# A hybrid decoder layer on one core: an account that meters the adding DMAs, a reordered head, a norm stepped at half tiles, and gate sigmoids ahead of silu

## The chip, the cores and the metric

The kernel runs on one core of a Trainium2 chip. The metric is device time in microseconds (us), the median of several executions. TensorE (PE) multiplies matrices, VectorE (DVE) and ScalarE (ACT) work elementwise, GpSimd (POOL) does a few small operations and issues one kind of DMA, and SyncE (SP) issues nearly all other DMAs. Every engine takes its instructions in the order in which the program lists them, and waits for other engines by semaphores.

## The reference

One layer for 256 tokens of width 1024, in float32: an RMS norm and one wide input projection, which feeds two branches; a gated mix of the branches; cross attention over 256 memory tokens; a squared-ReLU MLP; a last RMS norm. Cut to what matters here:

```python
n = rmsnorm(x);  z = n @ w_in      # c_a, c_g, q, k, v, qi, ki, wi, gc, ga
u = c_a * sigmoid(c_g)
u = causal depthwise conv of u, 31 taps, + conv_b
y_conv = silu(layernorm(u) * ln_g + ln_b) @ w_conv_out
y_attn = attention(q, k, v over the 64 best keys by the qi, ki, wi index) @ w_attn_out
h = x + (sigmoid(gc) * y_conv + sigmoid(ga) * y_attn) @ w_mix_out
h = h + cross_attention(rmsnorm(h), rmsnorm(mem))     # keys mem @ wx_kv, 4 heads
h = h + relu(rmsnorm(h) @ w_ff1)**2 @ w_ff2;  out = rmsnorm(h)
```

## The kernel before, in words

**Precision.** Almost every product is made of three: weights and activations are each split into a high part, rounded to the matmul's type, and a low rest. A weight chunk of 128 x 2048 (1 MB, tile `raw`) comes from memory; for each half of it ACT copies the high part (`hi`) and DVE subtracts to get the low part (`lo`). One "tile" of work on PE uses one such half: 8 matmuls of high weights on 512 columns (high and low activations) and 8 of low weights on 256.

**Streams.** `STREAM` lists the weight chunks in the order of use. `load()` issues the DMA of the next one on SP; three buffers of `raw` (and one in another pool) hold chunks, and a buffer's next load is issued when its low parts are done.

**Order.** All instructions are put in order while the program is built. `Counted` keeps for each of PE, DVE and ACT a running sum of estimated prices (`pe.total`, `dve.total`, `scalar.total`), and the builder compares these sums to decide what to put in next. After each PE tile come `meanwhile()` (optional work), the tile's own evacuation, and `tick()`, which steps every generator in `chains` once and counts `nturn`. The generators are the index scores, the heads of the attention, the layer norm, the gate's sigmoids. In order the tiles are: memory keys (`xk`), four pairs of `conv`, `qi`, `ki`, four more pairs of `conv`, `gc` (8 tiles), `v` (8), `q` and `k` in turn (16), `ga` (8), `ao` (8), `co` (8), `mix` (8), then cross attention and the MLP. The matmuls of `co` need the layer norm's result `u2`.

**The convolution.** Its 31 taps are shared out. Tap 0 is ACT's. Some are scalar_tensor_tensor on DVE, put in one by one from `fill` where `dve.total` allows. The others are *adds*: `Group.products` makes two ACT products of u and a tap's weights into the tile `prod` (one slot for each of the four groups of two channel tiles), and POOL issues a DMA that adds the 256 KB slot to the tile `added`. `ADDED` says how many taps of each group go that way: 11, 11, 10, 10, so 42 adds in all. A group may make its next product 3 turns after its last one, and `meanwhile` tries twice, so up to two products go in per tile. The slot must have been read by the last DMA before ACT overwrites it. When a half's taps are in and 3 turns have passed since its last product, `Half.add` sums `acc` and `added`; after both halves `layer_norm` starts: mean by a matmul (`ps_mub`), squares, inverse root (`rsqrt`, with a POOL power), silu on ACT, and high and low parts of `u2`, the high ones by a DVE copy. It waits for all heads, and the sigmoids of `ga` wait for its silu.

**The head of the program.** The vector of gains and biases (`vec`, 36 KB) is loaded on ACT's queue; SP loads half of the transposed memory (`mem_t`), half of chunk 0, the other halves, then rows of `x` and chunk 1. DVE multiplies all eight slices of `mem_t` by a gain, and then come the first matmuls `xk`. Eight matmuls on zeros (`ps_warm`) run before. The memory's own norm (`memory()`) ends with a POOL power `rs_m` and, one turn later, a PE transpose of it into `ps_mrb`.

Of the kernel before, what the change touches and what calls it, by code (L numbers as in the profile page):

```python
# [16 lines left out]
P = 128  # L17
# [8 lines left out]
ADDED = (11, 11, 10, 10)  # L26
# [80 lines left out]
def block_kernel(ctx, tc, x, xt, mem, memt, wst, wki, vecs, convw, gout, out):  # L107
# [75 lines left out]
    nload = [0]  # L183
    high_jobs, low_jobs = [], []

    def load(parts=1, before=lambda q: None):
# [57 lines left out]
    chains, fill, turn, done = [], [], [0], []  # L244
# [11 lines left out]
    def meanwhile():  # L256
# [5 lines left out]
        for _ in range(2):  # L262
            for g in groups:
                if g.ready() and scalar.total + 800 < pe.total + AHEAD:
                    g.products()
                    groups.remove(g)
                    groups.append(g)
                    break
# [4 lines left out]

    def tick():
        for c in list(chains):
            if next(c, "end") == "end":
                chains.remove(c)
# [97 lines left out]
    nc.scalar.dma_start(vec, vecs)  # L375
# [33 lines left out]
    for j in range(8):  # L409
# [87 lines left out]
    def memory():  # L497
# [11 lines left out]
        yield  # L509
# [32 lines left out]
    class Group:  # L542
# [5 lines left out]
        def ready(self):  # L548
            return self.open and self.left and nturn[0] >= self.issued + 3
# [11 lines left out]
    class Half:  # L561
# [18 lines left out]
        def add(self):  # L580
# [175 lines left out]
    u2 = []  # L756
# [3 lines left out]
    def layer_norm():  # L760
# [19 lines left out]
        dve.tensor_tensor(out=vs[:, 0, :], in0=vs[:, 0, :], in1=vs[:, 1, :], op=ALU.add)  # L780
        yield
        yield
        rs = rsqrt(vs[:, 0, :], "vr")
        yield
        while len(headed) < NH:
            yield
        act(table, table, AF.Silu)
        rsb = spread(rs, "rsb").unsqueeze(1).to_broadcast([P, 2, S])
        for c, cs in enumerate(pairs):
            dve.tensor_tensor(out=acc[:, cs, :], in0=acc[:, cs, :], in1=rsb, op=ALU.mult)  # L790
            for t in (2 * c, 2 * c + 1):
                act(acc[:, t, :], acc[:, t, :], AF.Silu, scale=lng[:, t : t + 1], bias=lnb[:, t : t + 1])
            if c == 1:
                yield
        gates.append(True)
        for c in range(4):
            parts_of(pairs[c])
            normed.append(True)
            if c != 1:
                yield  # L800

    def parts_of(cs):
        hi = u2[0].hi(cs.start, 2)
        dve.tensor_copy(hi, acc[:, cs, :])
        dve.tensor_tensor(out=u2[0].lo(cs.start, 2), in0=acc[:, cs, :], in1=hi.bitcast(F32), op=ALU.subtract)
# [5 lines left out]
    def head(h, q, k):  # L811
# [19 lines left out]
        yield  # L831
        for qb in range(2):
# [14 lines left out]
        headed.append(h)  # L847
# [19 lines left out]
    def gate_sigmoid():  # L867
        while not gates:
            yield
        act(table, table, AF.Sigmoid)  # L870
        for c in range(4):
            cs = slice(2 * c, 2 * c + 2)
            act(ga_t[:, cs, :], ga_t[:, cs, :], AF.Sigmoid)
            if c == 1:
                yield

    for i in range(4):
# [492 lines left out]
```

## Time and profile before

| | before |
|---|---|
| median of 3 runs | 522.6 us (521.56 to 524.28) |
| the profiled execution, its span | 525.86 us, 524.1 us |
| PE, DVE, ACT, POOL busy | 96%, 78%, 62%, 9% |
| bytes read from memory | 92.21 MB |

An engine's busy share is the mean over the whole span; what a stage costs is read from the waits inside it. "Granted clock" is the share of TensorE's full clock (2.4 GHz) that the chip let it have: 0.5 is 1.2 GHz.

### The profile page before, as it was taken

To read this page: it belongs to the slowest core of one execution; us is meant where nothing else is said; L and a number is where in the kernel's file an instruction comes from. 1 tells how busy PE (TensorE), PEld (TensorE's weight loads), DVE (VectorE), ACT (ScalarE), POOL (GpSimd) and SP (SyncE) were. 2 spreads that over 40 slices of the span, in tenths; PEclk is the share of its full clock that TensorE was granted. 3 is DMA by queue.
4 is the path that set the end of the run, shared out by engine and by line. 5 is a ranking of instruction groups with operands and counts; after the bars stand their busy time and mean duration, and the time that the engine had idled before them with its cause. 6 is when DMAs were issued, how large, how long until landed. Compare 5 with 4: busy or idle time off the path is not lost.

```text
span 524.1 us, 7696 instructions
## 1 busy us (share of the span) xinstructions
PE 505.6 (96%) x2876; PEld 442.2 (84%) x2876; DVE 407.2 (78%) x786; ACT 327.2 (62%) x595; POOL 45.2 (9%) x65
## 2 busy tenths in 40 slices
PE   8999899999959999999999999999999999999994
PEld 6999899888848898888888888988888888888883
DVE  2698999999869999689999985769666556666554
ACT  2665867776687876759669566556655545554432
POOL 1001222233332110000000000000000000000000
PEclk9999999999988999999999999999999999999999
DMA  8757989999999974453754454345555554565302
GB/s 305 282 229 230 283 210 227 229 239 252 256 258 252 239 202 161 162 222 110 303 199 165 151 193 185 120 161 180 223 203 198 199 202 161 179 222 175 148 0 80
DMA packets 20901, 104.76 MB, mean 200 GB/s; under 512 B 2432, under 2 KB 3328, under 8 KB 10496
## 3 DMA queue, kind: packets, MB, share of 16 engines
q1 hardware_dynamic: 14384, 92.90, 50.7%
q0 software_dynamic: 6048, 11.01, 11.7%
q8 instruction: 22, 0.36, 0.3%
q10 hardware_dynamic: 432, 0.36, 0.2%
q14 instruction: 15, 0.12, 0.1%
HBM read 92.21 MB, written 1.05 MB: 178 GB/s over the span
## 4 chain that ended last, share of the span: by engine, by line
PE 56%; DVE 22%; DMA 13%; ACT 5%; issue 3%; POOL 0%; POOLq 0%; DVEq 0%; ACTq 0%; SPq 0%
PE ps_f L88 17%; PE ps_ff L88 16%; DMA added<-prod 10%; DVE lo L88 8%; PE ps_ga L88 4%; DVE acc L88 3%; PE ps_xk L88 3%; PE ps_xo L88 2%; PE ps_k L88 2%; PE ps_xv L88 2%; DVE score L88 2%; PE ps_xq L88 2%; PE ps_ao L88 2%; DMA raw<-in_wst_dram 1%; DVE h_t L88 1%
## 5 line engine op out<-in xcount | busy, mean ns | idle before, releaser
L88 DVE TENSOR_TENSOR lo<-raw,hi 128x1024 fp32r<-128x1024 f32 (+1 forms) x161 | 195.0, 1216 | 5.9 <-ACT hi L88 5.9
L88 ACT ACTIVATE hi<-raw 128x1024 fp32r<-128x1024 f32 (+1 forms) x161 | 167.8, 1048 | 22.5 <-PE ps_ff L88 18.4
L88 PE MATMUL ps_ff<-hi,fs 128*128 128x512 f32 x256 | 81.7, 391 | 0.0
L88 PE MATMUL ps_f<-ff,hi 128*128 128x512 f32 x256 | 64.9, 393 | 0.2 <-DVE ff L88 0.2
L88 DVE SCALAR_TENSOR_TENSOR acc<-u,cw,acc 128x253 f32<-128x253 f32 (+18 forms) x148 | 62.2, 467 | 0.2
L88 PEld LDWEIGHTS ps_ff<-hi,fs 128*128 128x128 f32 x256 | 48.1, 188 | 9.7
L88 DVE TENSOR_TENSOR ft<-ps_f,ft 128x256 f32<-128x256 f32 x32 | 13.6, 425 | 53.9 <-ACT ft L88 53.9
L88 PEld LDWEIGHTS ps_f<-ff,hi 128*128 128x128 f32 x256 | 46.7, 188 | 9.8 <-DVE ff L88 1.1
L88 PE MATMUL ps_ff<-lo,fs 128*128 128x512 f32 x128 | 50.0, 390 | 0.0
L88 ACT ACTIVATE prod<-u,cw 128x226 f32<-128x226 f32 (+10 forms) x84 | 36.1, 477 | 20.2 <-DMA added<-prod 20.2
L557 POOL DMA_DIRECT2D added<-prod x42 | 36.5, 870 | 128.8 <-ACT prod L88 50.5
L88 PE MATMUL ps_conv<-n,hi 128*128 128x256 f32 x256 | 46.7, 285 | 0.0
L88 PEld LDWEIGHTS ps_conv<-n,hi 128*128 128x128 f32 x256 | 39.9, 192 | 0.8 <-issue 0.7
L88 PEld LDWEIGHTS ps_f<-ff,lo 128*128 128x128 f32 x256 | 35.1, 190 | 2.5
L88 PE MATMUL ps_conv<-n,lo 128*128 128x256 f32 x128 | 36.2, 283 | 0.0
L88 PE MATMUL ps_f<-ff,lo 128*128 128x256 f32 x256 | 36.0, 282 | 0.0
L88 ACT ACTIVATE fs<-ft 128x256 fp32r<-128x256 f32 x32 | 13.4, 419 | 31.2 <-DVE ft L88 31.2
L88 PEld LDWEIGHTS ps_ff<-lo,fs 128*128 128x128 f32 x128 | 24.1, 188 | 4.5
L88 ACT ACTIVATE ft<-ps_f 128x256 f32<-128x256 f32 x32 | 12.2, 380 | 22.5 <-PE ps_f L88 21.4
L88 PEld LDWEIGHTS ps_conv<-n,lo 128*128 128x128 f32 x128 | 24.5, 192 | 0.0
L88 PE MATMUL ps_q<-n,hi 128*128 128x512 f32 x64 | 18.4, 434 | 3.6 <-DVE q L88 3.6
L88 PE MATMUL ps_v<-hi,n 128*128 128x512 f32 x64 | 19.9, 389 | 0.0
(229 smaller groups left out, 870.2 us busy)
## 6 DMA issues: line engine op xcount, KB each, us to landing
raw<-in_wst_dram SPq DMA_DIRECT2D x79, 1024.0 KB, 4.9
added<-prod POOLq DMA_DIRECT2D x42, 256.0 KB, 7.9
raw<-in_wst_dram SPq DMA_DIRECT2D x6, 512.0 KB, 9.4
mem_t<-in_memt_dram SPq DMA_DIRECT2D x2, 512.0 KB, 5.5
x_rm<-in_x_dram SPq DMA_DIRECT2D x2, 512.0 KB, 9.0
mem_rm<-in_mem_dram SPq DMA_DIRECT2D x1, 1024.0 KB, 7.8
mem_t<-in_memt_dram SPq DMA_DIRECT2D x1, 1024.0 KB, 6.9
h_t<-in_xt_dram SPq DMA_DIRECT2D x1, 1024.0 KB, 8.3
```

Source lines behind the costliest of these rows:

```text
L88: return fn(*args, **kwargs)
L557: nc.gpsimd.dma_start(added[:, ts, :].rearrange("p t n -> p (t n)"), prod[:, self.n, :, :].rearrange("p t n -> p (t n)"), accum_op=ALU.add)
```

## The change

1. **Fewer adds, metered.** `ADDED` becomes 11, 10, 9, 8. An account `dma` sums DMA time: 1.3 ns for each column of a weight load, 1600 for each add, and never below `pe.total - 3000`. `meanwhile` makes one product at most, and only while the account stands under `pe.total + 500`. A group waits 3 turns while the account is under `pe.total - 1000`, otherwise 4, and a half ends 5 turns after its last product.
2. **The head.** `vec` is SP's first load. Chunk 0 comes as 512, 512 and 1024 columns; `mem_t`'s second half stands behind the first two of these. The multiplies of `mem_t` stand between the first matmuls. Nine matmuls on zeros. The transpose of `rs_m` comes four turns after its power.
3. **The norm.** `layer_norm` is in a new list, `urgent`, which `tick` steps and which is stepped once more in the middle of a tile of `form_b`. Its waits are restated in half tiles. The high parts of `u2` are ACT copies.
4. **Sigmoids first.** A head counts as done after its reciprocal. The sigmoids of `ga` start then, pair by pair, and silu waits for them.
5. **Small moves.** The sum of `ao`'s two halves is put in later (`lazily`); the scaling of the keys `kx` moves from the `ao` stage to just before `xq`.

```diff
-ADDED = (11, 11, 10, 10)
+ADDED = (11, 10, 9, 8)
...
-    nload = [0]
+    nload, dma = [0], [0.0]
...
-    def load(parts=1, before=lambda q: None):
+    def load(cuts=(0, N_CHUNK), before=lambda q: None):
...
-        for q in range(parts):
+        for q, ns in enumerate(slice(a, min(b, n)) for a, b in zip(cuts, cuts[1:])):
             before(q)
-            ns = slice(q * n // parts, (q + 1) * n // parts)
             nc.sync.dma_start(raw[:, ns], src[:, ns])
+            dma[0] += 1.3 * (ns.stop - ns.start)
...
-        for _ in range(2):
-            for g in groups:
-                if g.ready() and scalar.total + 800 < pe.total + AHEAD:
-                    g.products()
...
+        dma[0] = max(dma[0], pe.total - 3000)
+        for g in groups:
+            if g.ready() and scalar.total + 800 < pe.total + AHEAD and dma[0] < pe.total + 500:
+                dma[0] += 1600
+                g.products()
...
+    def step(some):
+        for c in list(some):
+            if next(c, "end") == "end":
+                some.remove(c)
+
     def tick():
...
+        step(chains)
+        step(urgent)
...
                 pe.matmul(ps, w[0][:, kt, :], x2.both(kt), start=kt == first, stop=False, skip_group_check=True)
+            step(urgent)
             for kt in kts:
...
-    nc.scalar.dma_start(vec, vecs)
+    nc.sync.dma_start(vec, vecs)
...
-        nc.sync.dma_start(mem_t[:, 4 * q : 4 * q + 4, :], memt[:, 4 * q : 4 * q + 4, :])
-
-    load(2, load_memory)
-    load(2, load_rows)
-    load(2)
+        if q in (0, 2):
+            nc.sync.dma_start(mem_t[:, 2 * q : 2 * q + 4, :], memt[:, 2 * q : 2 * q + 4, :])
+
+    load((0, 512, 1024, 2048), load_memory)
+    load((0, 1024, 2048), load_rows)
+    load((0, 1024, 2048))
...
-    for j in range(8):
+    for j in range(9):
         nc.tensor.matmul(ps, zero_r[:, :P], zero_r, start=True, stop=True)
...
-    for kt in range(KT):
-        dve.tensor_scalar(mem_t[:, kt, :], mem_t[:, kt, :], g_mem[:, kt : kt + 1], None, ALU.mult)
     psk = [ps_mm(f"ps_xk0{ct}") for ct in range(2)]
     for ct in range(2):
         for kt in range(KT):
+            if ct == 0:
+                dve.tensor_scalar(mem_t[:, kt, :], mem_t[:, kt, :], g_mem[:, kt : kt + 1], None, ALU.mult)
             mem_keys(psk[ct], 0, ct, kt)
...
-        yield
+        for _ in range(4):
+            yield
         act(mrb, spread(rs_m, "mrb"), AF.Copy)
...
-            return self.open and self.left and nturn[0] >= self.issued + 3
+            return self.open and self.left and nturn[0] >= self.issued + (3 if dma[0] < pe.total - 1000 else 4)
...
-                    p.left or not p.open or not (now or nturn[0] >= p.issued + 3) for p in self.groups):
+                    p.left or not p.open or not (now or nturn[0] >= p.issued + 5) for p in self.groups):
...
-                start(layer_norm())
+                urgent.append(layer_norm())
...
         dve.tensor_tensor(out=vs[:, 0, :], in0=vs[:, 0, :], in1=vs[:, 1, :], op=ALU.add)
-        yield
-        yield
+        for _ in range(4):
+            yield
         rs = rsqrt(vs[:, 0, :], "vr")
         yield
-        while len(headed) < NH:
+        yield
+        while gating[0] in chains:
             yield
         act(table, table, AF.Silu)
...
+            act(u2[0].hi(cs.start, 2), acc[:, cs, :], AF.Copy)
+            ready.append(scalar.total + 100)
+            if c < 3:
                 yield
-        gates.append(True)
...
     def gate_sigmoid():
-        while not gates:
+        while len(headed) < NH:
             yield
         act(table, table, AF.Sigmoid)
         for c in range(4):
+            while len(gates) < 2 * c + 2:
+                yield
...
     def after_ao(ct, ps):
-        total(ya[:, ct, :], ps)
-        due.append(lambda: added_up.append(ct))
+        act(ya[:, ct, :], ps[:, S:], AF.Copy)
...
     sq_x.fold(True)
+    dve.tensor_tensor(out=kx, in0=kx, in1=mrb.unsqueeze(1).to_broadcast([P, XH, S]), op=ALU.mult)
     scaled = start(cross_scale())
```

## Rows read from the trace of the kernel before

**Rows 1.** From the page: busy time of PE with its share of the span, and the granted clock in 40 equal slices, in tenths.

```profile
PE 505.6 (96%) x2876; PEld 442.2 (84%) x2876; DVE 407.2 (78%) x786; ACT 327.2 (62%) x595; POOL 45.2 (9%) x65
PEclk9999999999988999999999999999999999999999
```

**Rows 2.** The list of PE's waits: who waited for whom, us in total, how often, the longest.

```profile
PE ps_q L88 <- DVE q L88: 3.6, 1, 3.6
PE ps_s L88 <- DVE k L88: 2.3, 1, 2.3
...
PE ps_mrb L88 <- POOL rs_m L508: 1.6, 1, 1.6
...
PE ps_mub L88 <- ACT ptr L88: 0.6, 1, 0.6
...
PE ps_xq L88 <- DVE cx L88: 0.3, 1, 0.3
```

**Rows 3.** Two stretches, the end of the `v` tiles and the `q` and `k` tiles behind them: the stretch, its length, busy us (and instructions) of PE, PEld, DVE, ACT and POOL, then the mean granted clock, the busy share of the DMA engines and GB/s.

```profile
118.00:146.00 28.00, 27.47 (x137) 23.14 (x135) 23.84 (x45) 18.67 (x34) 8.65 (x11) 1.00 1.04 261
149.00:161.00 12.00, 9.66 (x38) 8.14 (x39) 10.89 (x23) 8.34 (x18) 3.87 (x5) 0.72 1.02 230
```

**Rows 4.** The waits between 118 and 146 us (first row), then single instructions of ACT and of PE in order of time: start, us, the instruction, and in brackets the idle time before it and what ended it.

```profile
ACT prod L88 <- DMA added<-prod: 9.3, 6, 3.9
...
144.73 0.87 ACT L88 ACTIVATE prod<-u,cw 128x230 f32<-128x230 f32 x2 [3.92 <-DMA added<-prod]
145.50 1.06 ACT L88 ACTIVATE v_rm<-ps_v 128x512 f32<-128x512 f32 x2
...
133.94 0.39 PE L88 MATMUL ps_v<-hi,n 128*128 128x512 f32 x1
...
149.05 2.74 PE L88 MATMUL ps_q<-n,hi 128*128 128x512 f32 x8 [3.58 <-DVE q L88]
```

**Rows 5.** From the page: the two large DMA queues (SP's and POOL's: packets, MB, the time of the packets as a share of 16 engines' span), and the DMA issues of the adds (count, KB each, median us from issue to landing).

```profile
q1 hardware_dynamic: 14384, 92.90, 50.7%
q0 software_dynamic: 6048, 11.01, 11.7%
...
added<-prod POOLq DMA_DIRECT2D x42, 256.0 KB, 7.9
```

**Rows 6.** The adds by stretch: the stretch, its length, POOL's time in them and their number, the granted clock, the share of the DMA engines and GB/s.

```profile
96.00:118.00 22.00, 6.07 (x7) 1.00 0.97 243
118.00:146.00 28.00, 7.89 (x10) 1.00 1.04 261
```

**Rows 7.** The head: single instructions of ACT's queue, DVE and PE in order of time; two stretches of 4 us with PE's busy time and number of matmuls first; and from the page the landing of `vec` (KB, us).

```profile
0.74 0.41 ACTq L375 DMA_DIRECT2D vec<-in_vecs_dram  x1
...
5.09 1.14 DVE L88 TENSOR_SCALAR mem_t<-mem_t,vec 128x256 f32<-128x256 f32 x4 [3.23 <-DMA vec<-in_vecs_dram]
8.54 1.14 DVE L88 TENSOR_SCALAR mem_t<-mem_t,vec 128x256 f32<-128x256 f32 x4 [2.30 <-DMA mem_t<-in_memt_dram]
...
1.92 3.78 PE L410 MATMUL ps_warm<-zero_r 128*128 128x512 f32 x8 [1.92 <-DVE zero_r L395]
6.30 12.60 PE L88 MATMUL ps_xk<-mem_t,raw 128*128 128x256 f32 x48 [0.60 <-DVE mem_t L88]
...
6.30:10.30 4.00, 4.00 (x10) 3.20 (x11) 1.14 (x4) 0.00 (x0) 0.00 (x0) 1.00 0.96 360
10.30:14.30 4.00, 4.00 (x20) 3.54 (x19) 0.91 (x2) 1.81 (x3) 0.55 (x1) 1.00 1.02 415
...
vec<-in_vecs_dram ACTq DMA_DIRECT2D x1, 36.0 KB, 4.3
```

**Rows 8.** The memory's norm on POOL and PE, single instructions in order of time.

```profile
56.36 0.72 POOL L508 TENSOR_TENSOR rs_m<-ss_m,half 128x2 f32<-128x2 f32 x1 [1.93 <-DMA added<-prod]
...
57.13 0.43 PE L88 MATMUL ps_mrb<-ident,rs_m 128*128 128x128 f32 x2 [1.63 <-POOL rs_m L508]
```

**Rows 9.** Prices: four DVE taps in a row (start, us); then groups of equal instructions with their count, busy us and mean ns of one; and from the chain of waits in order of time two tiles of PE (start, us).

```profile
127.15 1.63 DVE L88 SCALAR_TENSOR_TENSOR acc<-u,cw,acc 128x249 f32<-128x249 f32 x4
...
L88 ACT ACTIVATE prod<-u,cw 128x226 f32<-128x226 f32 (+10 forms) x84 | 36.1, 477 | 20.2 <-DMA added<-prod 20.2
L88 DVE CAST u<-acc 128x512 fp32r<-128x512 f32 x4 | 1.7, 420 | 0.0
L88 DVE TENSOR_TENSOR kv<-kv,mrb 128x1024 f32<-128x1024 f32 x1 | 1.2, 1218 | 0.0
...
208.61 5.59 PE ps_ga L88 x32
```

**Rows 10.** The layer norm: single instructions of DVE, ACT and PE from the sum of the second half to the first matmul of `co`.

```profile
205.95 1.23 DVE L88 TENSOR_TENSOR acc<-acc,added 128x1024 f32<-128x1024 f32 x1
210.19 0.89 DVE L88 TENSOR_TENSOR usum<-usum 128x256 f32<-128x256 f32 x2
...
235.15 1.28 ACT L88 ACT_TABLE_LOAD   x1
...
247.52 0.69 DVE L88 TENSOR_TENSOR u<-acc,u 128x512 fp32r<-128x512 f32 x1
...
248.75 2.00 PE L88 MATMUL ps_co<-u,hi 128*128 128x512 f32 x8
```

**Rows 11.** DVE at the cross attention's scores, one instruction.

```profile
303.98 0.69 DVE L88 TENSOR_REDUCE xmx<-ps_xs 128x2 f32<-128x512 f32 x1 [1.08 <-PE ps_xs L88]
```

More of the change, by code (lines that the diff above doesn't have):

```diff
@@ L241, in weights @@
         return [w.rearrange("p (k n) -> p k n", k=kt) for w in prepared.pop(key)]
-    chains, fill, turn, done = [], [], [0], []
+    chains, urgent, fill, turn, done = [], [], [], [0], []
     waiting = [False]
@@ L261, in meanwhile @@
             later.pop(0)()
-        for _ in range(2):
-            for g in groups:
-                if g.ready() and scalar.total + 800 < pe.total + AHEAD:
-                    g.products()
-                    groups.remove(g)
-                    groups.append(g)
-                    break
+        dma[0] = max(dma[0], pe.total - 3000)
[3 more added lines that the diff above has]
+                g.products()
+                groups.remove(g)
+                groups.append(g)
+                break
         while may_fill() and dve.total < pe.total + AHEAD:
@@ L272, in meanwhile @@
             g.finish()
+    def step(some):
+        for c in list(some):
+            if next(c, "end") == "end":
+                some.remove(c)
     def tick():
-        for c in list(chains):
-            if next(c, "end") == "end":
-                chains.remove(c)
+        step(chains)
+        step(urgent)
         nturn[0] += 1
@@ L753, in block_kernel @@
         form_a("v", hf, n2, v_rm, (1.0, 1.0))
-    u2 = []
+    u2, gating = [], []
     normed = []
@@ L788, in layer_norm @@
         rsb = spread(rs, "rsb").unsqueeze(1).to_broadcast([P, 2, S])
+        ready = []
         for c, cs in enumerate(pairs):
             dve.tensor_tensor(out=acc[:, cs, :], in0=acc[:, cs, :], in1=rsb, op=ALU.mult)
+            scalar.after(dve.total + 100)
             for t in (2 * c, 2 * c + 1):
                 act(acc[:, t, :], acc[:, t, :], AF.Silu, scale=lng[:, t : t + 1], bias=lnb[:, t : t + 1])
-            if c == 1:
+            act(u2[0].hi(cs.start, 2), acc[:, cs, :], AF.Copy)
+            ready.append(scalar.total + 100)
+            if c < 3:
                 yield
-        gates.append(True)
-        for c in range(4):
-            parts_of(pairs[c])
-            normed.append(True)
-            if c != 1:
-                yield
[L802 to L805, printed above, removed]
+        for c, cs in enumerate(pairs):
+            for _ in range(4):
+                if pe.total < ready[c]:
+                    yield
+            dve.after(ready[c])
+            dve.tensor_tensor(out=u2[0].lo(cs.start, 2), in0=acc[:, cs, :], in1=u2[0].hi(cs.start, 2).bitcast(F32),
+                              op=ALU.subtract)
+            normed.append(True)
     o2 = Pair("o")
@@ L831, in head @@
         yield
+        headed.append(h)
         for qb in range(2):
@@ L871, in gate_sigmoid, with gate_attention @@
         for c in range(4):
+            while len(gates) < 2 * c + 2:
+                yield
             cs = slice(2 * c, 2 * c + 2)
             act(ga_t[:, cs, :], ga_t[:, cs, :], AF.Sigmoid)
-            if c == 1:
-                yield
+            yield
+    def gate_attention(ct, ps):
+        total(ga_t[:, ct, :], ps, bga[:, ct : ct + 1])
+        due.append(lambda: gates.append(ct))
+    gating.append(start(gate_sigmoid()))
     for i in range(4):
-        form_b("ga", i, n2, lambda ct, ps: total(ga_t[:, ct, :], ps, bga[:, ct : ct + 1]))
-    gating = start(gate_sigmoid())
+        form_b("ga", i, n2, gate_attention)
     for c in heads:
@@ L884, in block_kernel, with add, lazily @@
     memorised = start(memory_parts())
-    added_up = []
+    added_up, lazy = [], []
     def after_ao(ct, ps):
-        total(ya[:, ct, :], ps)
-        due.append(lambda: added_up.append(ct))
+        act(ya[:, ct, :], ps[:, S:], AF.Copy)
+        ready, turn_of = scalar.total + 100, nturn[0]
+        def add():
+            dve.after(ready)
+            dve.tensor_tensor(out=ya[:, ct, :], in0=ps[:, :S], in1=ya[:, ct, :], op=ALU.add)
+            added_up.append(ct)
+        lazy.append((ready, turn_of, add))
+    def lazily(force=False):
+        while lazy and (force or lazy[0][0] < max(dve.total, pe.total) or nturn[0] > lazy[0][1] + 2):
+            lazy.pop(0)[2]()
     def branches():
-        dve.tensor_tensor(out=kx, in0=kx, in1=mrb.unsqueeze(1).to_broadcast([P, XH, S]), op=ALU.mult)
-        while gating in chains:
+        while gating[0] in chains:
             yield
         for ct in range(KT):
+            lazily()
             while ct >= len(added_up):
                 yield
+                lazily()
             dve.tensor_tensor(out=ga_t[:, ct, :], in0=ya[:, ct, :], in1=ga_t[:, ct, :], op=ALU.mult)
@@ L905, in block_kernel @@
         form_b("ao", i, o2, after_ao)
+        lazily()
+    lazily(True)
     while fill:
```

3 lines of the change are left out of this document (1 added, 2 removed).

## The prediction

> **What bounds the kernel now.** I read the page first. PE is busy 96% of the span, and its granted clock is full but for two slices [rows 1]. So nothing but PE's idle time and its slow time can be won: 524.1 - 505.6 = 18.5 us idle, of which some 7 us are the tail behind the last matmul, which the change leaves alone.
>
> The second view is the list of PE's waits [rows 2]. Its two longest, 3.6 us for `q` and 2.3 us for `k`, are both for evacuations of the attention's projections. The third view is the stretch in which they lie: from 149 to 161 us the granted clock is 0.72, and the DMA engines are at 1.02 [rows 3]. At that clock (1 - 0.72) x 12 = 3.4 us are lost; the short idle pieces in it fall mostly at full clock, and I count 3.2. Together this place costs 3.6 + 2.3 + 3.2 = 9.1 us.
>
> The fourth view says why. Between 118 and 146 us ACT stood 9.3 us waiting to overwrite a `prod` slot that an add's DMA had not yet read, once for 3.92 us [rows 4]. The last matmul of `v` began at 133.94 us, yet ACT copied `v` out at 145.50, some 11 us later. PE ran four more tiles into free banks and then stood until the first `q` had been taken out, 149.05 us. The cause is DMA time. SP's queue took 50.7% of the span for 92.90 MB, so 0.507 x 524.1 / 92.90 = 2.86 us per MB, 3.0 us per chunk of 1.05 MB, 1.5 us per tile; the 42 adds took 0.117 x 524.1 / 42 = 1.46 us each [rows 5]. Two tiles of PE take 5.59 us [rows 9], so a tile leaves 2.8 - 1.5 = 1.3 us, room for 0.9 adds. In the ten tiles from 118 to 146 us ten adds went out, of which PE's idle time at the end is a part; the program had packed them into the eight tiles of `v` [rows 6]. Eight tiles have room for 7.
>
> **Part 1, adds.** Products per tile fall from at most two to one, in `v` from 10 to at most 8. The excess over the room falls from (10 - 7) x 1.46 = 4.4 us of DMA time to 1.5. With four groups taking turns a slot is reused after four tiles, 11.2 us, against a median of 7.9 us from issue to landing [rows 5]. In `q` and `k`, 38 - 12 - 7 - 8 = 11 adds are left (12 went out before the row at 96 us, 7 in it) for 16 tiles, which have room for 14. So ACT's lag of 11 us should shrink by about 9.3 - 1.5 = 7.8 us, to 3 to 4 us, and PE bears four tiles of lag before it stands. I take 8.8 of the 9.1 us as won. The bounds are 9.1 and 0, if the DMA engines stay saturated and the lag builds up anyway.
>
> One rule of the Trainium skill would take this gain away. DMA: Bandwidth & Descriptors, "Anatomy of one DMA", fits a POOL-queued transfer as 2.0 us plus bytes over 436 GB/s, 2.6 us for an add; on that count a slot is free long before three turns (8.4 us), nothing is to be metered, and this part is worth 0. The same page, "Queues, rings and completion order", lets each engine turn in order between the rows that have work. The median of 7.9 us agrees with the second: the adds stand beside the weights.
>
> What part 1 adds: 4 adds are 8 DVE taps, at 1.63 / 4 = 0.41 us [rows 9], 3.3 us. They lie in `fill`, beside PE. DVE has 28 - 23.8 = 4.2 us free in one stretch [rows 3], and the change takes two things off it before `co`: four high copies (1.7 us) and `kx` (1.2 us) [rows 9]. Net 0.4 us; cost 0 while cover holds, 3.3 us if it is gone. ACT loses 8 products of 0.48 us and gains 4 copies, at the 0.53 us of the `v` copies [rows 4, 9], so 1.7 us less.
>
> **Part 2, head.** The first matmul `xk` starts at 6.30 us. From there to 10.3 us PE finishes 10 matmuls, in the next 4 us 20 [rows 7]. The clock column says 1.00 for both, as no change is recorded before it; the pace says 1.2 GHz, then 2.4. Before, PE stood 0.60 us between the zeros and `xk`. A ninth zero matmul at 3.78 / 8 = 0.47 us fills most of that, and the first `xk` needs 512 columns where it needed 1024. `vec` now stands ahead of SP's other loads and moves each of their issues by 0.41 us; behind nothing it should land sooner than 4.3 us, and I take the first multiply at 5.4 us and `xk` near 5.9. Without a gap the clock may rise before 10.3 us, worth up to 2.0 us. But the second half of `mem_t`, multiplied from 8.54 us, still comes behind the same number of bytes, and the fifth `xk` waits for it: it began at about 9.85 and can begin at 8.9. From there on PE is at full clock in either case. So 1.1 us (0.9 there, 0.2 on the matmul after it). Bounds: -0.4 if all loads only shift, and 2.4.
>
> On this the Trainium skill (TensorE: Matmul & The Clock Gate, "Part 1: The HAM clock gate") says that the low clock is the default, that activity releases it, and that the moment varies between runs. The pace at 6.3 us agrees; the varying moment no row here can show. By it the head may give 0 in one run and 2 in another.
>
> The memory norm's transpose: PE waited 1.63 us for a POOL power that itself stood behind an add's landing for 1.93 us [rows 8]. The power stays where it is; the transpose and its ACT copy move three tiles, 8.4 us, and nobody needs `mrb` before `kx`. Gain 1.6 us; if what stands behind PE is late anyway, 0.
>
> **Parts 3 and 4, norm and sigmoids.** Before, the second half was summed at 205.95 us, its mean's sums stood at 211.1, silu's table was loaded at 235.15, the last `u2` was written at 248.2 and `co` began at 248.75 without a wait [rows 10]: 0.5 us to spare. By my count of turns the second half now ends up to three tiles later (5 turns instead of 3, and 6 of the 8 taps, which go in at 2 to 3 per tile). The half-tile steps win two back before silu and let `u2` follow in 1.5 tiles instead of three. Silu comes at the same tile as before, the sigmoids (two table loads either way) are done by then. Cost 0, bounds -0.6 (the wait of `ps_mub`) and +3. The mean's matmul comes one tile after its sums instead of three: DVE wrote them 3.2 us after PE's tile, so it fits by a hair. Queued behind a late one on PE would be the rest of that tile.
>
> **Part 5.** `kx`, 1.22 us, now stands on DVE ahead of low weights and `qx`; DVE had 1.08 us free before the first score maximum [rows 11], so 0.2 us is lost. The later `ya` sums hide under `ao`.
>
> **The sum.** 8.8 + 1.1 + 1.6 - 0.2 = 11.3 us. The profiled execution took 525.86 us, so 514.6 there. It stands 3.3 us above the median of the runs, 522.6; from that, 511.3 us.
>
> **Rivals.** A, the metering is too weak. For it: DMA was at 1.02 to 1.04 throughout [rows 3], and one add per tile is still over 0.9. Against it: 11 adds instead of 15 are left for `q` and `k`. If half the 9.1 us or all of it stays: 522.6 - 2.5 - (4.6 to 0) = 515.5 to 520.
>
> B, all waits go and the clock rises early: 9.1 + 2.4 + 1.6 + 0.6 = 13.7, so 509. For it: each has a row; against it, the fixed bytes at the head.
>
> C, slower: the adds are starved. The account holds a product back, the second half's sum comes late, and the norm's chain stands bare between `ao` and `co`. The place is that sum. The chain behind it, from 205.95 to 248.2 us, is 15 tiles long [rows 10]; half-tile steps make it about 12, an estimate, so three tiles of lateness are free. From there each tile costs PE 2.8 us, and with 11.3 / 2.8 = 4 more the gain is gone: it decides at a sum seven tiles late, in the second tile of `ao`. Four tiles behind that point the time is 522.6 + 4 x 2.8 = 534. Against it: the account grows by 1331 + 1600 per tile and PE's sum by about 2770, so it lets 0.9 adds per tile pass; 38 need 42 tiles of the 57 before `ga` ends.
>
> D, no change: the static order meets the same lag elsewhere, 521 to 524.
>
> **How the numbers follow.** Forecast (509.5 to 514) 0.57, B 0.10, A 0.20, D 0.07, C 0.06. The range 508 to 518.5 leaves out C, D, the worst of A and a little of B, 0.2 together. What a measurement can tell from no change is about 0.5%, 2.6 us. Faster (under 520.0): 0.87. Within: 0.07. Slower: 0.06.
>
> **What would show it.** Right: no PE wait for `q` or `k` over 1 us and full clock from 140 to 170 us; ACT's wait for adds between 118 and 146 us under 3 us; `v` copied out within 5 us of its last matmul; `xk` starting before 6.0 us and `pt_n` about 1 us earlier than 18.7; no wait at `ps_mrb`; no wait at the first `co`. Wrong: a PE wait at `co` or at `ps_mub`, adds issued during `ao`, or an ACT lag in `v` as long as before.

## The result, and the profile after

The changed kernel takes 517.0 us (median of 20 runs, 514.6 to 522.8), the kernel before, beside it, 523.8 us (20 runs, 521.6 to 528.0). The ratio is 0.987 with an interval of 0.984 to 0.990: 6.8 us faster, 5.4 to 8.2. The forecast was faster by 11.3, to 511.3, with a range up to 518.5. The direction was right and the time lies in the range; the gain is 60% of what was forecast. The profiled execution took 517.7 us, 8.2 less than the profiled one of before; that pair is taken apart first.

From the page of the changed kernel: span, PE, clock; two DMA queues; landings (count, KB each, us).

```profile
span 515.9 us, 7683 instructions
PE 502.9 (97%) x2877; PEld 439.9 (85%) x2877; DVE 408.0 (79%) x790; ACT 325.9 (63%) x591; POOL 41.7 (8%) x61
PEclk9999999999999999999999999999999999999998
...
q1 hardware_dynamic: 14672, 92.94, 50.7%
q0 software_dynamic: 5472, 9.96, 10.9%
...
added<-prod POOLq DMA_DIRECT2D x38, 256.0 KB, 8.3
raw<-in_wst_dram SPq DMA_DIRECT2D x5, 512.0 KB, 10.9
mem_t<-in_memt_dram SPq DMA_DIRECT2D x2, 512.0 KB, 6.4
```

PE's work is 2.7 us shorter (it ran at full clock almost throughout) and its idle time 5.5 us shorter than in [rows 1]. The two slices in which the clock was down are gone. The weights moved as much as before, the adds are four fewer, and an add still lands after some 8 us.

The list of PE's waits, whole (who waited for whom, us in total, how often, the longest):

```profile
PE ps_xk L88 <- DVE mem_t L88: 3.0, 2, 2.7
PE ps_warm L417 <- DVE zero_r L402: 1.9, 1, 1.9
PE ps_s L88 <- DVE k L88: 0.6, 1, 0.6
PE ps_co L88 <- DVE u L88: 0.3, 1, 0.3
PE ps_f L88 <- DVE ff L88: 0.2, 1, 0.2
```

Against [rows 2]: the waits for `q`, for the power at `ps_mrb` and at `ps_mub` are gone, the one for `k` fell from 2.3 to 0.6. There is a new one on top, of 2.7 us, for `mem_t`, in the head.

Where the pair differs is read from the start of each stage's first matmul (the timeline of PE; us):

| first matmul of | before | after | difference | change within the stage ahead |
|---|---|---|---|---|
| conv | 23.75 | 26.81 | +3.06 | +3.06 (head) |
| ki | 60.20 | 61.20 | +1.00 | -2.06 (`ps_mrb` lies in it) |
| q | 134.17 | 135.40 | +1.23 | +0.23 |
| ga | 196.76 | 189.01 | -7.75 | -8.98 (`q` and `k`) |
| ao | 225.72 | 217.10 | -8.62 | -0.87 (`ps_mub` lies in it) |
| co | 248.75 | 240.13 | -8.62 | 0 |
| mix | 271.09 | 263.07 | -8.02 | +0.60 |
| f | 337.35 | 329.21 | -8.14 | -0.12 |
| end of the span | 524.08 | 515.91 | -8.17 | -0.03 |

So nearly everything came at one place, `q` and `k`, and a third of it was given back in the first 27 us.

**The place that was won.** First the stretches of [rows 3] in the changed kernel (same columns), then ACT's waits for adds from 118 to 146 us.

```profile
118.00:146.00 28.00, 28.00 (x138) 23.68 (x137) 27.22 (x54) 22.43 (x41) 9.79 (x11) 1.00 1.05 282
149.00:161.00 12.00, 11.42 (x66) 9.92 (x65) 11.93 (x31) 10.13 (x26) 3.44 (x4) 1.00 1.07 295
...
ACT prod L88 <- DMA added<-prod: 4.3, 2, 2.4
```

The DMA engines are as full as before (1.05 and 1.07), and from 118 to 146 us there are again ten adds. What changed stands in ACT's own order. Single instructions of ACT behind the first copy of `v` (start, us), then PE's last for `v`:

```profile
128.52 1.07 ACT L88 ACTIVATE v_rm<-ps_v 128x512 f32<-128x512 f32 x2
132.97 0.87 ACT L88 ACTIVATE prod<-u,cw 128x230 f32<-128x230 f32 x2 [2.43 <-DMA added<-prod]
...
136.69 0.86 ACT L88 ACTIVATE prod<-u,cw 128x229 f32<-128x229 f32 x2 [1.90 <-DMA added<-prod]
...
138.41 0.85 ACT L88 ACTIVATE prod<-u,cw 128x233 f32<-128x233 f32 x2
...
140.13 1.05 ACT L88 ACTIVATE v_rm<-ps_v 128x512 f32<-128x512 f32 x2
...
135.17 0.39 PE L88 MATMUL ps_v<-hi,n 128*128 128x512 f32 x1
```

Between its two copies of `v` ACT now has three pairs of products. Before it had five there (at 133.86, 136.02, 137.28, 139.01 and 144.73 us), behind a first copy at

```profile
131.96 1.06 ACT L88 ACTIVATE v_rm<-ps_v 128x512 f32<-128x512 f32 x2
```

So from copy to copy ACT takes 11.6 us instead of 13.5; its waits there are as long as they were (4.3 us, 4.7 before), it is the two pairs that are gone. The larger part was won ahead of the first copy. It comes 14.9 us behind the first matmul of `v` (113.61 us) instead of 19.6 (112.38 us before). Behind ACT's last instruction for `gc` four pairs stand ahead of it instead of five, and none of them waits for an add, where before three waits took 4.7 us. The second copy comes 140.13 - 135.17 = 5.0 us behind PE instead of 11.6 [rows 4]. That is below the four tiles of PE that fit into free banks (11.3 us in the kernel before, from 134.17 to where PE stopped at 145.47), so PE never stands for `q`.

**The place that was lost.** The head of the changed kernel: DVE, then PE, then the stretches of [rows 7] with PE's busy time and matmuls, granted clock, DMA share and GB/s.

```profile
5.50 1.14 DVE L88 TENSOR_SCALAR mem_t<-mem_t,vec 128x256 f32<-128x256 f32 x4 [3.64 <-DMA mem_t<-in_memt_dram]
11.27 1.14 DVE L88 TENSOR_SCALAR mem_t<-mem_t,vec 128x256 f32<-128x256 f32 x4 [4.63 <-DMA mem_t<-in_memt_dram]
...
6.40 2.60 PE L88 MATMUL ps_xk<-mem_t,raw 128*128 128x256 f32 x8 [0.28 <-DVE mem_t L88]
11.68 10.29 PE L88 MATMUL ps_xk<-mem_t,raw 128*128 128x256 f32 x40 [2.68 <-DVE mem_t L88]
21.80 1.91 PE L88 MATMUL pt_n<-ident,x_rm 128*128 128x128 f32 x16
...
6.30:10.30 4.00, 2.60 (x8) 1.00 0.92 296
10.30:14.30 4.00, 2.62 (x6) 0.60 1.03 420
```

The second half of `mem_t` was multiplied at 11.27 us instead of 8.54 [rows 7]. PE stood 2.68 us for it, and behind that gap the granted clock was 0.60 where it was full in the kernel before: six matmuls in four microseconds instead of twenty. The 48 matmuls of `xk` took 21.97 - 6.40 = 15.6 us instead of 12.6.

### The profile page after: what moved, and what is told of

It reads as the page before. It is cut to its first block, busy times and chain, and to the rows that moved or that the text cites. A ratio compares the mean times of both kernels' runs of the same rounds, so it can differ in the third digit from the quotient of the medians.

```text
span 515.9 us, 7683 instructions
## 1 busy us (share of the span) xinstructions
PE 502.9 (97%) x2877; PEld 439.9 (85%) x2877; DVE 408.0 (79%) x790; ACT 325.9 (63%) x591; POOL 41.7 (8%) x61
## 3 DMA queue, kind: packets, MB, share of 16 engines
HBM read 92.21 MB, written 1.05 MB: 181 GB/s over the span
## 4 chain that ended last, share of the span: by engine, by line
PE 64%; DVE 23%; DMA 5%; ACT 5%; issue 2%; SPq 0%; POOLq 0%; POOL 0%; DVEq 0%; ACTq 0%
PE ps_f L88 17%; PE ps_ff L88 16%; DVE lo L88 9%; DVE acc L88 5%; PE ps_ga L88 4%; PE ps_mix L88 3%; PE ps_k L88 3%; PE ps_q L88 3%; PE ps_xk L88 3%; PE ps_xo L88 2%; DMA added<-prod 2%; PE ps_xq L88 2%; PE ps_xv L88 2%; DVE score L88 2%; DMA mem_t<-in_memt_dram 2%
## 5 line engine op out<-in xcount | busy, mean ns | idle before, releaser
L88 DVE SCALAR_TENSOR_TENSOR acc<-u,cw,acc 128x244 f32<-128x244 f32 (+18 forms) x156 | 65.7, 468 | 0.2
L565 POOL DMA_DIRECT2D added<-prod x38 | 33.1, 871 | 118.2 <-ACT prod L88 38.4
L88 ACT ACTIVATE prod<-u,cw 128x226 f32<-128x226 f32 (+10 forms) x76 | 32.5, 475 | 8.3 <-DMA added<-prod 8.3
L88 PE MATMUL ps_xk<-mem_t,raw 128*128 128x256 f32 x64 | 16.5, 419 | 3.0 <-DVE mem_t L88 3.0
```

The source lines that it names most:

```text
L88: return fn(*args, **kwargs)
L565: nc.gpsimd.dma_start(added[:, ts, :].rearrange("p t n -> p (t n)"), prod[:, self.n, :, :].rearrange("p t n -> p (t n)"), accum_op=ALU.add)
```

## Experiments

Each ratio is against the kernel before on the same chip, whose median there was between 523.7 and 524.1 us. It is the ratio on record and need not be the quotient of the two medians: for a_vecact that quotient is 0.989 and the ratio 0.985. The kernels named `a_` are the changed kernel with one thing put back, those named `b_` the kernel before with one thing of the change.

### The account and the one product per tile

**a_oldmeter**: two tries per tile, no account, a slot again after three tiles; the 38 adds stay.

```diff
-        for g in groups:
-            if g.ready() and scalar.total + 800 < pe.total + AHEAD and dma[0] < pe.total + 500:
-                dma[0] += 1600
-                g.products()
...
+        for _ in range(2):
+            for g in groups:
+                if g.ready() and scalar.total + 800 < pe.total + AHEAD:
+                    g.products()
...
-            return self.open and self.left and nturn[0] >= self.issued + (3 if dma[0] < pe.total - 1000 else 4)
+            return self.open and self.left and nturn[0] >= self.issued + 3
```

> The changed kernel without the account (two tries per tile, three turns), still 38 adds. Theory that the limit of one product per tile did it: ACT's lag and PE's wait for q come back at least in part, 4 to 9 us slower than the changed kernel, ACT's wait for adds between 118 and 146 us over 6 us. Rival, that four adds fewer were enough: within 1.5 us of the changed kernel.

Measured: 524.7 us, ratio 1.003 (1.000 to 1.006), so 7.7 us above the changed kernel. In its profile (PE's waits, then ACT's from 118 to 146 us) the old waits are back:

```profile
PE ps_s L88 <- DVE k L88: 3.4, 1, 3.4
...
PE ps_q L88 <- DVE q L88: 1.8, 1, 1.8
...
ACT prod L88 <- DMA added<-prod: 7.6, 5, 2.6
```

Between ACT's copies of `v` (at 131.21 and 143.56 us) there are five pairs again, and the granted clock falls behind the wait for `k`. Fewer adds alone don't win the place; where they stand in ACT's order does.

**a_onlyone** keeps the one product per tile without the account, **a_two** the account with two tries per tile.

```diff
-            if g.ready() and scalar.total + 800 < pe.total + AHEAD and dma[0] < pe.total + 500:
+            if g.ready() and scalar.total + 800 < pe.total + AHEAD:
...
-            return self.open and self.left and nturn[0] >= self.issued + (3 if dma[0] < pe.total - 1000 else 4)
+            return self.open and self.left and nturn[0] >= self.issued + 3
```

```diff
-        for g in groups:
-            if g.ready() and scalar.total + 800 < pe.total + AHEAD and dma[0] < pe.total + 500:
+        for _ in range(2):
+            for g in groups:
+                if g.ready() and scalar.total + 800 < pe.total + AHEAD and dma[0] < pe.total + 500:
...
```

> The changed kernel with one product per tile but without the account and with three turns. Theory (the limit of one per tile is what matters, four groups in turn make four turns of it): within 1.5 us of the changed kernel. Rival (the account and the fourth turn matter): 3 to 8 us slower, waits for q or k above 1 us.

> The changed kernel with its account and its three or four turns, but two tries per tile. Theory (one per tile is what matters): 3 to 8 us slower, as without any metering (524.7). Rival (the account holds the rate by itself): within 1.5 us of the changed kernel.

Measured: a_onlyone 519.4 us (0.993, 0.989 to 0.996), a_two 518.5 us (0.989, 0.986 to 0.993). Either half wins most of it, so neither is the cause alone; the theory of a_two, that one product per tile is what matters, did not hold, and a_onlyone lies between its theory and its rival. What they share is seen in ACT's order. Pairs of products between ACT's last instruction for `gc` and its second copy of `v`, and how far that copy comes behind the first matmul of `v` (us):

| | pairs | second copy | median |
|---|---|---|---|
| before | 10 | 33.1 | 523.8 |
| a_oldmeter | 10 | 31.3 | 524.7 |
| a_onlyone | 8 | 27.9 | 519.4 |
| a_two | 7 | 27.0 | 518.5 |
| changed | 7 | 26.5 | 517.0 |

The last three medians are too close to be told apart; the intervals of their ratios overlap. In the profiles of a_onlyone and a_two PE waits 2.3 us for `k`, in the changed kernel 0.6. In the five other variants that keep the whole of part 1 and of the norm it waits 0 to 1.6 us, but in b_adds (below) 2.3 again: that the two halves together also keep `k` clear is not shown.

### The count of adds and the steps of the norm

**a_oldadded**: the changed kernel with the 42 adds of before. **a_nohalf**: the changed kernel without the step of the norm in the middle of a tile.

```diff
-ADDED = (11, 10, 9, 8)
+ADDED = (11, 11, 10, 10)
```

```diff
-            step(urgent)
             for kt in kts:
                 pe.matmul(ps[:, :S], w[1][:, kt, :], x2.hi(kt), start=False, stop=kt == last, skip_group_check=True)
```

> The changed kernel with 42 adds again (11, 11, 10, 10), metered. Theory (the metering did it): no PE wait for q, but the halves end one to two tiles later and the norm with them; 0 to 3 us slower than the changed kernel, at co. Rival (the count did it): 4 us or more slower, with PE waits at q and k.

> The changed kernel without the step in the middle of a tile, so the norm moves once per tile with waits written for half tiles. Theory (the half tiles are needed to make room for part 1): the norm ends three to five tiles later, PE waits at co, 8 to 14 us slower than the changed kernel. Rival (there was room): within 1.5 us of it.

The norm's waits are written for half tiles, so without that step each of them lasts twice as long: a_nohalf has a slower norm than the kernel before, not the same one. The cleaner test of part 1 without the new norm is the next kernel.

**b_adds**: the kernel before with part 1 alone (38 adds, account, one per tile, five turns before a sum).

```diff
-ADDED = (11, 11, 10, 10)
+ADDED = (11, 10, 9, 8)
...
-        for _ in range(2):
-            for g in groups:
...
+        for g in groups:
+            if g.ready() and scalar.total + 800 < pe.total + AHEAD and dma[0] < pe.total + 500:
+                dma[0] += 1600
...
-                    p.left or not p.open or not (now or nturn[0] >= p.issued + 3) for p in self.groups):
+                    p.left or not p.open or not (now or nturn[0] >= p.issued + 5) for p in self.groups):
```

> The kernel before with part 1 alone: 38 adds, the account, one product per tile, 5 turns before a half ends. Theory: the 9 us at q and k are won, but the norm, stepped once per tile, starts two to three tiles later and part of it comes back as a PE wait at co: 2 to 7 us faster than before in all, with a wait at co of 2 us or more. Rival (the norm has room): 8 to 9 us faster, no wait at co.

Measured: a_oldadded 528.7 us (1.010, 1.006 to 1.015), a_nohalf 530.8 us (1.011, 1.008 to 1.015), b_adds 523.3 us (0.998, 0.995 to 1.000). All three lose it behind `ao`; for a_oldadded that is neither its theory (0 to 3 us) nor its rival (waits for `q` and `k`). These are single instructions of PE at `co` in a_nohalf, and then the stretch from 236 to 258 us (columns as in [rows 3]):

```profile
243.66 1.19 PE L88 MATMUL ps_co<-u,hi 128*128 128x512 f32 x2 [4.61 <-DVE u L88]
...
249.79 1.19 PE L88 MATMUL ps_co<-u,hi 128*128 128x512 f32 x2 [3.35 <-DVE u L88]
...
236.00:258.00 22.00, 13.47 (x53) 10.03 (x52) 13.55 (x24) 14.57 (x27) 0.00 (x0) 0.69 0.26 96
```

in b_adds:

```profile
242.31 0.73 PE L88 MATMUL ps_co<-u,hi 128*128 128x512 f32 x2 [1.56 <-DVE u L88]
...
246.89 1.22 PE L88 MATMUL ps_co<-u,hi 128*128 128x512 f32 x2 [2.78 <-DVE u L88]
...
236.00:258.00 22.00, 17.33 (x84) 14.17 (x83) 18.92 (x38) 15.89 (x29) 0.00 (x0) 0.84 0.46 176
```

and in a_oldadded:

```profile
236.05 0.43 PE L88 MATMUL ps_rsb<-ident,rs_vr 128*128 128x128 f32 x2 [2.34 <-POOL rs_vr L422]
...
248.03 3.19 PE L88 MATMUL ps_co<-u,hi 128*128 128x512 f32 x6 [4.78 <-DVE u L88]
```

In the changed kernel the same stretch has 21.67 us of PE and a full clock, and the norm answers to [rows 10] like this (DVE's sum of the second half and its mean's sums, silu's table on ACT, PE at the mean and at `co`):

```profile
206.69 1.23 DVE L88 TENSOR_TENSOR acc<-acc,added 128x1024 f32<-128x1024 f32 x1
...
212.75 0.89 DVE L88 TENSOR_TENSOR usum<-usum 128x256 f32<-128x256 f32 x2
...
226.93 1.28 ACT L88 ACT_TABLE_LOAD   x1
...
213.87 0.60 PE L88 MATMUL ps_mub<-usum,onesd 128*128 128x256 f32 x2
...
240.13 1.55 PE L88 MATMUL ps_co<-u,hi 128*128 128x512 f32 x6
```

There the sum lies 217.10 - 206.69 = 10.4 us ahead of `ao`; before it was 19.8 us ahead, so it has come 9.4 us closer, 3.4 tiles. It still suffices, because silu's table is loaded 13.2 us ahead of `co`. From the five profiles (us):

| | sum ahead of `ao` | sum to silu's table | `ao` to `co` | `ao` to `mix` |
|---|---|---|---|---|
| before | 19.8 | 29.2 | 23.0 | 45.4 |
| b_adds | 10.0 | 28.2 | 23.5 | 53.4 |
| changed | 10.4 | 20.2 | 23.0 | 46.0 |
| a_nohalf | 10.2 | 34.2 | 28.0 | 58.6 |
| a_oldadded | 0.4 | 18.7 | 26.8 | 56.2 |

In b_adds the sum comes late and the chain keeps its old length; in a_nohalf the sum is no later than in the changed kernel, but the chain is 14.0 us longer (5.0 longer than before); in a_oldadded the chain is short, but the sum comes ten us later. Where `u` comes in pieces PE stops between matmuls, and then the clock falls too: behind `co`'s first matmul a_nohalf takes 30.7 us to `mix` where the changed kernel takes 22.9.

What makes the sum late differs. In the changed kernel and in b_adds it is the eight taps that DVE took over, not the metered adds: the last add goes out at 178.91 us, 38.2 us ahead of `ao` (32.3 before), and the sum follows the last tap at once.

```profile
202.96 1.21 DVE L88 SCALAR_TENSOR_TENSOR acc<-u,cw,acc 128x236 f32<-128x236 f32 x3
...
206.21 0.45 DVE L88 SCALAR_TENSOR_TENSOR acc<-u,cw,acc 128x234 f32<-128x234 f32 x1
```

The first row is the last of the taps before (they end 21.6 us ahead of `ao`), the second that of the changed kernel (10.4 us ahead). In a_oldadded the taps end early (192 us) and the metered adds late (the last goes out at 199.3 us).

Part 1 in the kernel before (b_adds) takes 56.8 us from `q`'s first matmul to `ga`'s instead of 62.6, and 53.4 from `ao`'s to `mix`'s instead of 45.4: it wins 5.8 us and gives 8.0 back. So part 1 alone wins nothing, and a shorter chain is what lets its gain through; the cut of the count is needed too. How much of the shorter chain is the half-tile steps, the sigmoids or the copies on ACT, no run tells apart.

### The head

**a_oldhead** puts the whole head back (`vec` on ACT's queue, pieces of 1024 columns, the eight multiplications in front, eight zeros).

```diff
-    nc.sync.dma_start(vec, vecs)
+    nc.scalar.dma_start(vec, vecs)
...
-    load((0, 512, 1024, 2048), load_memory)
+    load((0, 1024, 2048), load_memory)
...
-    for j in range(9):
+    for j in range(8):
...
+    for kt in range(KT):
+        dve.tensor_scalar(mem_t[:, kt, :], mem_t[:, kt, :], g_mem[:, kt : kt + 1], None, ALU.mult)
...
```

**b_newhead** is the reverse of this diff in the kernel before.

```diff
-    nc.scalar.dma_start(vec, vecs)
+    nc.sync.dma_start(vec, vecs)
...
-    load(2, load_memory)
+    load((0, 512, 1024, 2048), load_memory)
...
-    for j in range(8):
+    for j in range(9):
...
```

> The changed kernel with the head of before (vec on ACT's queue, two 1024-column pieces, eight multiplies in front, eight zero matmuls). Theory: the new head costs what its profile shows, 3 us at the first conv matmul (26.81 against 23.75), so this runs 2 to 4 us faster than the changed kernel, 513 to 515, with the first conv near 23.8. Rival: the late second half of mem_t was the luck of one execution; then it is within 1 us of 517, or 1 us slower.

> The kernel before with the new head alone. Theory: 2 to 4 us slower than before, the fifth xk matmul again after 11 us. Rival (luck, and my prediction of a gain of 1.1): 0 to 1.5 us faster than before.

Measured: a_oldhead 517.0 us (0.986, 0.982 to 0.991), the same median as the changed kernel (the 2 to 4 us less that were expected did not come, though its profile has conv at 22.75 us); b_newhead 526.1 us (1.003, 1.000 to 1.006), 1.4 us slower than before by its ratio. So the head gains nothing, and in the kernel before it tends to cost. In the profile of a_oldhead PE reads:

```profile
6.25 1.97 PE L88 MATMUL ps_xk<-mem_t,raw 128*128 128x256 f32 x8 [0.85 <-DVE mem_t L88]
9.00 8.90 PE L88 MATMUL ps_xk<-mem_t,raw 128*128 128x256 f32 x40 [0.78 <-DVE mem_t L88]
17.74 1.91 PE L88 MATMUL pt_n<-ident,x_rm 128*128 128x128 f32 x16
```

The wait is 0.78 instead of 2.68 us. **a_coarse** puts only the pieces of 1024 columns back, **a_vecact** only `vec` on ACT's queue, and **a_coarsevec** both, so that of the new head the ninth zero and the interleaved multiplications are left.

```diff
...
-    load((0, 512, 1024, 2048), load_memory)
+    load((0, 1024, 2048), load_memory)
```

```diff
-    nc.sync.dma_start(vec, vecs)
+    nc.scalar.dma_start(vec, vecs)
```

> The changed kernel with chunk 0 in two pieces of 1024 columns, mem_t's second half between them (vec still SP's first load, nine zero matmuls, multiplies between the matmuls). Theory: the two 512-column pieces hold up the DMA engines, so here mem_t's second half lands near 9 us instead of 11.2, the first conv matmul starts near 23 us in the profile, and the time is 1 to 3 us under the changed kernel's 517.0. Rival (vec on SP is what delays): mem_t still lands after 10.5 us, time as the changed kernel's.

> The changed kernel with vec back on ACT's queue, chunk 0 still in 512, 512 and 1024 columns. Theory (the pieces): mem_t's second half lands after 10.5 us as in the changed kernel, time within 1.5 us of it. Rival (vec): it lands near 8.7 us, time 1 to 3 us less.

> The changed kernel with chunk 0 in two pieces of 1024 columns and vec back on ACT's queue; only the ninth zero matmul and the interleaved multiplies are left of the new head. Theory: mem_t's second half lands near 8.5 us, no PE wait over 1 us in xk, first conv matmul at 22.5 to 23.5 us in the profile; the best version, 515 to 516.5 in time. Rival (the head does not show in runs without the profiler, as old head and coarse pieces gave 517.0 and 517.2): 517 within 1 us.

Measured: a_coarse 517.2 us (0.984, 0.980 to 0.989), a_vecact 518.1 us (0.985, 0.979 to 0.990), a_coarsevec 515.0 us (0.983, 0.979 to 0.987). The 1 to 3 us less that were expected of a_coarse did not come. The last is the fastest of all kernels run, 2.0 us below the changed one; the intervals overlap. Its head (DVE, PE, then the first stretch of [rows 7]):

```profile
5.11 1.14 DVE L88 TENSOR_SCALAR mem_t<-mem_t,vec 128x256 f32<-128x256 f32 x4 [3.25 <-DMA vec<-in_vecs_dram]
8.54 1.14 DVE L88 TENSOR_SCALAR mem_t<-mem_t,vec 128x256 f32<-128x256 f32 x4 [2.29 <-DMA mem_t<-in_memt_dram]
...
6.32 11.53 PE L88 MATMUL ps_xk<-mem_t,raw 128*128 128x256 f32 x48 [0.19 <-DVE mem_t L88]
17.69 1.91 PE L88 MATMUL pt_n<-ident,x_rm 128*128 128x128 f32 x16
...
6.30:10.30 4.00, 3.98 (x14) 1.00 0.94 364
```

In four profiles with the loads of before (before, a_oldhead, b_adds, a_coarsevec) the second half of `mem_t` is multiplied at 8.54 to 8.59 us, in the seven with the whole new head at 9.05 to 11.27, median 10.82. With one of the two edits there is one profile each, and both times lie between:

```profile
9.24 1.14 DVE L88 TENSOR_SCALAR mem_t<-mem_t,vec 128x256 f32<-128x256 f32 x4 [2.72 <-DMA mem_t<-in_memt_dram]
...
10.01 1.14 DVE L88 TENSOR_SCALAR mem_t<-mem_t,vec 128x256 f32<-128x256 f32 x4 [3.89 <-DMA mem_t<-in_memt_dram]
```

The first is `vec` on SP alone (a_coarse), the second the fine pieces alone (a_vecact). So the two edits of the loads cost this time; how it is shared between them, single profiles can't tell.

PE runs its 48 matmuls in a_coarsevec without a stop, and `pt_n` comes at 17.69 us, 1.0 us ahead of before. But it comes at 17.74 in a_oldhead and at 17.69 in b_adds, which have the old head. So this microsecond is not shown to be won by any edit: two of the three profiles with the old head have it too, and the kernel before, in the one execution from which the forecast was made, had not.

### The memory norm's transpose

**a_nomrb** puts the transpose back to one turn behind the power.

```diff
-        for _ in range(4):
-            yield
+        yield
         act(mrb, spread(rs_m, "mrb"), AF.Copy)
```

> The changed kernel with one turn instead of four between the memory norm's power and its transpose. Theory: PE's wait at ps_mrb of 0.7 to 1.8 us comes back and the time rises by as much, 517.7 to 519. Rival: PE is held by something else soon after and nothing is lost, 517 within 0.5.

Measured: 518.6 us (0.991, 0.988 to 0.995), 1.5 us above the changed kernel in the median. But its profile has no wait at `ps_mrb` (the transpose runs at 55.63 us), and from conv's first matmul to `ki`'s it takes 34.73 us, only 0.34 more than the changed kernel. The power comes 2.8 us behind the start of an add's issue on POOL in every one of these profiles (53.56 to 56.36 us before, 52.06 to 54.85 in a_nomrb); what moved is that add, which lies 28.1 us behind `conv`'s first matmul in a_nomrb and 29.8 before. In b_adds, where the transpose is also where it was, that is 28.9, and PE waits 0.7 us. So the wait depends on where an add happens to lie, between 0 and 1.6 us, and the move takes the chance away. That the move itself is worth 1.5 us is not shown: the ratios' intervals overlap, and the one profile gives 0.34.

## Why the prediction was right or wrong

**Part 1 was right in its place and size, and in the main in its cause.** `q` and `k` gave 9.0 us in the profiled pair, 8.8 were forecast, with the clock's share in it. ACT's wait from 118 to 146 us was to be under 3 us and is 4.3; `v` was to be copied out within 5 us, and is. The working counted room in DMA time: ten pairs in `v`, at most eight behind the change, room for seven; there are seven. The rate did not fall, though: the traces show as many adds and as full DMA engines as before from 118 to 146 us. What fell is how many products stand in ACT's order ahead of the second copy of `v`, and it takes fewer of these landings to get there. The Trainium skill's fit of a POOL-queued transfer (DMA: Bandwidth & Descriptors, "Anatomy of one DMA") gave this part nothing, as an add would land, by an estimate from it, in 2.6 us. The trace disagrees: 8.3 us, and without the metering 7.7 us are lost.

**The head is the step that failed.** The prediction let the second half of `mem_t` come "behind the same number of bytes" and so no later, and put 1.1 us with a lower bound of -0.4. Behind the same bytes it was multiplied 2.7 us later, and the profiled head cost 3.06: a miss of 4.2 us in the profiled pair, more than the whole shortfall of 3.1 there (514.6 forecast, 517.7 found). The changed kernel's profile is one of the worst heads: in the profiles of the changed kernel and of its six variants with the whole new head conv starts between 23.96 and 26.81 us, median 24.98; in the three with the old one (before, a_oldhead, b_adds) between 22.70 and 23.75, median 22.75. That is 2.2 us lost where 1.1 was to be won. The timed medians show less, nothing (a_oldhead) to 1.4 us (b_newhead), each uncertain by 1.5 to 2.4 us. How much of 2.2 an unprofiled run pays stays open. The early start of `xk`, "near 5.9", did not come either (6.40; 5.92 to 6.75 in the seven profiles). And the 1.1 us was priced on one execution in which full pace came late: the fifth slice's matmuls, at 9.85 there and forecast at 8.9, start at 9.00 in a_oldhead and 8.95 in b_adds with the old head, so most of that gain was there without the change.

**The transpose**, 1.6 forecast: 2.06 in the stage that holds it, of which 1.63 is the wait that went. The size came out, but not shown by the move: a_nomrb has no wait either, and only 0.34 us of the 2.06 come back there. That the power stood behind an add's landing, as the prediction reads the row, is doubtful: POOL is idle for the same 1.92 to 1.93 us in the changed kernel, b_adds and a_nomrb, where the row names another releaser, and an add lands only after some 8 us.

**Norm and sigmoids**, at 0: right for the kernel as a whole (`co` waits 0.3 us, `mub` has no wait), and the count of "up to three tiles later" was 3.4. But the cost of 0 is the balance of two large things: with the old norm part 1 gives back 8.0 us (b_adds), and with the new norm stepped once per tile the kernel is 13.8 us slower (a_nohalf). Of the two reasons given for the late sum the taps are the one that binds; the five turns are over before them. The chance of 0.06 for rival C looked at the second sum alone and put its point of decision seven tiles late; the mechanism already shows at 3.4 tiles when the chain is not also shortened (b_adds). No margin is left there: `co` waits 0.3 us.

**Rival A** gave the time that came (515.5 to 520), by another cause: the metering was strong enough. (Its "11 adds instead of 15" left for `q` and `k` should have read 13: 42 - 12 - 7 - 10.) Rival D, the same lag elsewhere, is what b_adds shows: `co` takes over from `q`. Rival B fell with the head.

**`kx`**, -0.2: `mix` to `f` took 0.1 us less, so it cost nothing that shows.

**From the profiled pair to the median.** The forecast took the pair's gain over to the median unchanged. The pair gained 8.2 us, the medians 6.8, and the profiled execution of before lay 2.1 us above its median of 20 runs. Of the 4.5 us that are missing (11.3 - 6.8) 3.1 stand in the profiled pair, from the head; 1.4 are between the pair and the medians, within the interval of the ratio, and no profile here assigns them.

## What to carry to other kernels

An engine that both feeds a slow DMA and empties another engine's banks must have few such feeds ahead of each emptying: count what stands in its queue ahead of the copy, not the rate. A gain behind which a chain has half a microsecond to spare is only worth what that chain lets through, so shorten the chain in the same change, and test the two apart. Cutting the first loads finer to start sooner can delay the load behind them; look at when the second one lands.

## What the runs showed of the hardware

The new loads moved fewer bytes per second in the head. From 4 to 6 us the DMA engines moved 392 GB/s in the kernel before, 384 in a_coarsevec, and 264 in the changed kernel, at a busy share of 0.85; from 6 to 8 us 272, 277 and 206. With the smaller pieces alone (a_vecact) the first figure is 308, with `vec` on SP alone (a_coarse) 354. In the packet records the two pieces of 512 columns go as 256 packets of 2 KB, most of them in 0.1 us, but the last eleven start between 7.0 and 9.3 us, up to four microseconds behind the middle one (5.4), and `mem_t`'s second half, queued behind the second of these pieces, is the load that PE waits for. It is not so in each execution: in a_nomrb, with the same head, the last of the 256 starts at 6.82 us, and `mem_t`'s second half is multiplied at 9.05. The Trainium skill (DMA: Bandwidth & Descriptors, "Measured (HBM→SBUF, 128 partitions, SWDGE, issued from GpSimd)") says that transfers should be gathered to 1 MiB for three quarters of the peak, and has 138 GB/s at 64 KB. It measured transfers that GpSimd queues; these are SP's. It speaks against cutting 512 KB into two of 256 KB, and the direction agrees here; the prediction didn't weigh it.

The same head had PE on a different pace in two profiles. In the kernel before, 10 matmuls ran from 6.3 to 10.3 us [rows 7]. In a_oldhead, with the same head, 14 did, though PE stood idle for 0.78 us of them, and `pt_n` came 1.0 us sooner. So the moment at which the clock rises is worth a microsecond by itself, about what the head was to win. The Trainium skill (TensorE: Matmul & The Clock Gate, "Part 1: The HAM clock gate") says that this moment varies between runs; here the traces agree, where those of before alone could not show it.

A stop of PE cost more than its length wherever it was followed by a low clock: behind 2.68 us in the head the granted clock was 0.60 for 4 us, and in a_nohalf, with 8.5 us of waits for `u`, the stretch from `ao` to `mix` took 58.6 instead of 46.0 us. Not every stop was followed by one: in a_oldmeter PE stood 3.23 us at the same place of the head, and the granted clock from 10.3 to 14.3 us stayed at 1.00.
